# A two-layer decoder trunk in split fp32: seven-product blocks that end with two plain pairs, a gate chain moved into the second block, and another order for the residual adds

## The chip, the cores and the metric

The kernel runs on one core of a Trainium2 chip. The metric is the device time of one execution in microseconds. The profile used here was taken of one execution of the kernel before; times in it are counted from the start of its span. PE is the tensor engine (PEld its weight loads), DVE the vector engine, ACT the scalar engine, POOL GpSimd, SP the engine that issues most of the DMA transfers.

## The reference

The input is 256 tokens of width 2048 in fp32. Layer 0 mixes an mLSTM and a Mamba-2 state-space part behind one combined input projection, layer 1 is attention; each is followed by a SwiGLU of width 5632. Cut to the frame:

```python
for layer in range(DEPTH):
    xn = rms_norm(x, norm_mix[layer])
    if layer % 2 == 0:
        x = x + mixer_mlstm_ssd(xn, *mixer_params[layer])
    else:
        x = x + mixer_moba(xn, *mixer_params[layer])
    x = x + swiglu(rms_norm(x, norm_ffn[layer]), *ffn_params[layer])
return rms_norm(x, final_norm)

def swiglu(x, w_gate, w_up, w_down):
    return (jax.nn.silu(x @ w_gate) * (x @ w_up)) @ w_down
```

In layer 0, `proj = xn @ w_in` holds q, k, v, o of eight mLSTM heads, two gate columns per head, and z, x, B, C and dt of the state-space part. The gates (8 + 8 + 32 columns) go through log-sigmoid, softplus, a running sum and a running maximum before the rest can use them as decays. The two results are joined and go through `w_out`.

## The kernel before

**Blocks.** Every projection is a `block` (L254): 256 tokens against two strips of 512 columns, so four results of 128 tokens x 512 columns in four PSUM banks `F[0..3]` (in the profile `acc_f`). The 2048 rows of a weight matrix are taken in eight pairs of 256 rows (j = 0 to 7). A plan, a string with a letter per pair (`PLAN`, L36), says how a pair is multiplied. Each fp32 factor is split into a high part and a remainder in fp32r, and each product of two such is three matmuls (L262 to L264, `add`).

- P, plain: 4 results x 2 row tiles x 3 = 24 matmuls of 128x512.
- S, seven products (a 2x2 scheme of the Strassen kind): 7 x 3 = 21 matmuls. Three products go straight into `F`, four into extra banks `E` (`acc_e`), which after the last S of the block are folded into four tiles `pre` (L295 on ACT, L296 to L299 on DVE). S needs sums of weights (DVE L244, L246, L247, L249) and sums of activations (`activation_sums`, L210: four small DVE operations on `sf`, then a split on ACT and DVE into `sk`).

**Weights.** `weights` (L226) starts two DMAs of 512 KB per pair from SP, then for every piece a cast on ACT (`wh`, L235) and the remainder on DVE (`wl`, L236). There are 6 buffers each of `raw`, `wh` and `wl`, so the two engines can run ahead of PE only as far as six buffers reach (a P takes two of each, an S four `wh` and four `wl`).

**Sums of activations.** They are made in one of two places: where the activations are turned (`transpose_split`, L187, when pair j is listed in `kt.sums`), or late, when the first S that needs them is reached (`summed`, L178, with an extra add `xg` at L183). In the input `xt0`, in `sx`, `mx` and `o` they are made late; in the inputs of the SwiGLUs (`xt1`, `xt3`), of layer 1 (`xt2`) and in the hidden activations (`ha`, `hb`) where they are turned.

**Order of the work.** Work that belongs to one block and is done during the next is handed to `later` (L142) with a number of pairs to wait; `tick` (L153) runs what is due after every pair, but nothing from the first S of a block to its last (`held`, L139). `need` runs what is still due of a name. A scheduler then orders each engine by the program's order and by the priorities given (`tc.high_priority`: 800 for weights, 1600 for draining banks).

**Blocks in order.** bc0, bc1, xz0 to xz3, qk0 (projection `w_in`), w1.0, w1.1 (`w_out`, state-space half), v0, o0, qk1, v1, o1 (`w_in`), w2.0, w2.1 (`w_out`, mLSTM half), the first SwiGLU (eleven hidden blocks ah0 to ah10, with down blocks ad0, ad4, ad8 of two halves between them), av0, aq0, aq1, av1, aq2, aq3, wo.0, wo.1 (layer 1), and the second SwiGLU (bh0 and so on). These names are the text's; each stands for one call of `block`.

**Around the change.** The gate chain (L432 to L487) stands in line between bc0 and `bc_done(0, FB)` at L562, which drains the banks of bc0 through `scaled` (L537, tile `tok`, on ACT). `project` (L750) adds a `w_out` or `w_o` block to the residual `xin`: `add_all` (L755) adds the four `pre` right after the last S, and the four `F` at the block's end.

Of the kernel before, what the change touches and what calls it, by code (L numbers as in the profile page):

```python
# [60 lines left out]
def hybrid_trunk(ctx: ExitStack, tc: tile.TileContext, a: dict, out: bass.AP):  # L61
# [370 lines left out]
    pg = aux_bank("p_gate")  # L432
    for k in range(KD):
        xh, xl = xt0.parts(k)
        wgh, wgl = wgp[k // 8]
        nc.tensor.matmul(pg[:96, :T], wgh[:, k % 8, :], xh, start=k == 0, stop=False)
        nc.tensor.matmul(pg[:96, :T], wgh[:, k % 8, :], xl, start=False, stop=False)
        nc.tensor.matmul(pg[:96, :T], wgl[:, k % 8, :], xh, start=False, stop=k == KD - 1)
    gate = t2([96, T], "gate")
    nc.vector.tensor_mul(gate, pg[:96, :T], rb0[:96])  # L440
    gv = t2([64, T], "gv")
    nc.vector.tensor_scalar(gv, gate[0:64], gbias[0:64], sgn, op0=OP.add, op1=OP.mult)
    u = t2([8, T], "u")
    nc.vector.tensor_scalar(u, gate[64:72], gbias[64:72], None, op0=OP.add)
    ab = t2([64, T], "ab")
    nc.vector.scalar_tensor_tensor(ab, gv, -1.0, gv, op0=OP.mult, op1=OP.max)
    nc.scalar.activation(ab, ab, AF.Exp, scale=-1.0)
    den = t2([64, T], "den")
    nc.vector.tensor_scalar(den, ab, 2.0, None, op0=OP.add)
    nc.vector.reciprocal(den, den)  # L450
    zz = sk_home([64, 4, T], "zz")
    z, z2, pp, sp = zz[:, 0, :], zz[:, 1, :], zz[:, 2, :], zz[:, 3, :]
    nc.vector.tensor_mul(z, ab, den)
    nc.vector.tensor_mul(z2, z, z)
    nc.vector.tensor_scalar(pp, z2, 1.0 / 17, None, op0=OP.mult)
    for n in (15, 13, 11, 9, 7, 5, 3):
        nc.vector.scalar_tensor_tensor(pp, pp, 1.0 / n, z2, op0=OP.add, op1=OP.mult)
    nc.vector.scalar_tensor_tensor(pp, pp, 1.0, z, op0=OP.add, op1=OP.mult)
    nc.vector.tensor_scalar(gv, gv, 0.0, None, op0=OP.max)
    nc.vector.scalar_tensor_tensor(sp, pp, 2.0, gv, op0=OP.mult, op1=OP.add)  # L460
    ga = t2([64, T], "ga")
    nc.vector.tensor_scalar(ga, sp, lam, None, op0=OP.mult)
    cum = t2([64, T], "cum")
    one_t = t2([64, T], "one_t")
    nc.gpsimd.memset(one_t, 1.0)
    nc.vector.tensor_tensor_scan(cum, one_t, ga, 0.0, op0=OP.mult, op1=OP.add)
    colsrc = t2([P, T], "colsrc")
    nc.gpsimd.memset(colsrc, 0.0)
    nc.vector.tensor_sub(colsrc[0:8], u, cum[0:8])
    cmx = t2([8, T], "cmx")  # L470
    nc.vector.tensor_tensor_scan(cmx, colsrc[0:8], colsrc[0:8], 0.0, op0=OP.max, op1=OP.max)
# [514 lines left out]
```

## Time and profile before

| | us |
|---|---|
| median of 3 runs (2648.64 to 2652.11) | 2651.81 |
| the profiled execution | 2650.01 |
| its span in the trace | 2648.2 |
| PE busy, share of the span | 2572.2, 97% |
| PE weight loads busy | 2106.0, 80% |
| DVE busy | 2284.2, 86% |
| ACT busy | 1528.7, 58% |
| mean DMA rate | 187 GB/s |

A busy PE is not a PE at full pace: matmuls overlap, and at a lower granted clock the same matmul is longer. So the table of busy times says which engines are nearly always occupied, and not how much a stage could give. What a stage could give is read by stretches: the time from the first matmul of a block to that of the next, beside what each engine did in it and the clock that PE was granted. Blocks with the same plan should last the same; where one lasts longer, the timeline of PE shows a start that waited, with the time idle and its releaser in square brackets.

### The profile page before, as it was taken

The page shows a single profiled execution, that of the slowest core. Times are in us where ns is not written, and L with a number is a line of the kernel's source. Part 1 is how long each engine was busy: PE and PEld are TensorE (multiplying, and loading weights), DVE is VectorE, ACT ScalarE, POOL GpSimd, SP SyncE. Part 2 cuts the span into 40 slices and gives each one's busy share as a digit, 9 for nine tenths or more (in the row PEclk, how much of TensorE's full clock was granted, in tenths as well). Part 3 has the DMA queues.
Part 4 walks back from the last instruction along what each step waited for, and adds up shares of the span by engine and source line. Part 5 has one row for each costly group of instructions (what it writes and reads, how often), then busy time and mean ns, then how long its engine had stood idle before and what let it go on. Part 6 is the DMA issues. An engine that isn't in the chain of part 4 may idle for free.

```text
span 2648.2 us, 32709 instructions
## 1 busy us (share of the span) xinstructions
PE 2572.2 (97%) x11630; PEld 2106.0 (80%) x11630; DVE 2284.2 (86%) x3097; ACT 1528.7 (58%) x2052; POOL 59.6 (2%) x97
## 2 busy tenths in 40 slices
...
GB/s 270 138 177 184 184 176 182 183 175 191 179 157 176 192 213 186 202 196 198 190 199 198 187 187 202 146 178 182 140 174 196 196 207 185 207 191 201 198 214 135
DMA packets 254835, 494.51 MB, mean 187 GB/s; under 512 B 16024, under 2 KB 16544, under 8 KB 254672
## 3 DMA queue, kind: packets, MB, share of 16 engines
...
q14 instruction: 72, 0.59, 0.1%
...
## 4 chain that ended last, share of the span: by engine, by line
PE 75%; DVE 11%; issue 8%; DMA 4%; ACT 2%; POOL 1%; ACTq 0%; POOLq 0%; SPq 0%; DVEq 0%
PE acc_f L263 20%; PE acc_f L262 20%; PE acc_f L264 20%; DVE wl L236 5%; PE acc_e L262 4%; PE acc_e L263 4%; PE acc_e L264 4%; ACT wh L235 1%; PE p_tr L192 1%; DMA raw<-in_l_ffn_up 1%; DMA raw<-in_l_ffn_down 1%; DMA raw<-in_l_w_qkv 1%; DVE sums L244 1%; DVE raw L246 1%; DVE sums L247 1%
## 5 line engine op out<-in xcount | busy, mean ns | idle before, releaser
L235 ACT CAST wh<-raw 128x1024 fp32r<-128x1024 f32 (+1 forms) x1049 | 1030.1, 996 | 809.4 <-PE acc_f L264 493.8
L236 DVE TENSOR_TENSOR wl<-raw,wh 128x1024 fp32r<-128x1024 f32 (+1 forms) x1049 | 1197.0, 1151 | 260.2 <-ACT wh L235 252.8
L262 PE MATMUL acc_f<-wh,x 128*128 128x512 f32 x1324 | 520.2, 394 | 9.5 <-DVE xin L757 9.5
L263 PE MATMUL acc_f<-wl,x 128*128 128x512 f32 x1324 | 518.3, 391 | 1.2 <-DVE wl L236 1.2
L264 PE MATMUL acc_f<-wh,x 128*128 128x512 f32 x1324 | 518.5, 392 | 0.0
L262 PEld LDWEIGHTS acc_f<-wh,x 128*128 128x128 f32 x1324 | 249.6, 188 | 61.4 <-issue 6.6
L262 PE MATMUL acc_f<-wh,xa 128*128 128x512 f32 x696 | 278.5, 401 | 15.6 <-ACT tok L537 12.0
L263 PEld LDWEIGHTS acc_f<-wl,x 128*128 128x128 f32 x1324 | 249.7, 189 | 53.9 <-DVE wl L236 3.2
L264 PEld LDWEIGHTS acc_f<-wh,x 128*128 128x128 f32 x1324 | 249.6, 188 | 52.0
L263 PE MATMUL acc_f<-wl,xa 128*128 128x512 f32 x696 | 274.0, 394 | 1.9 <-DVE wl L236 1.9
L264 PE MATMUL acc_f<-wh,xa 128*128 128x512 f32 x696 | 274.4, 394 | 0.0
L236 DVE TENSOR_TENSOR wl<-sums,wh 128x1024 fp32r<-128x1024 f32 x137 | 167.0, 1219 | 9.8 <-ACT wh L235 8.9
L235 ACT CAST wh<-sums 128x1024 fp32r<-128x1024 f32 x137 | 143.7, 1049 | 43.9 <-PE acc_f L264 17.6
L262 PE MATMUL acc_e<-wh,sk 128*128 128x512 f32 x411 | 166.0, 405 | 1.7 <-ACT wh L235 0.8
L262 PEld LDWEIGHTS acc_f<-wh,xa 128*128 128x128 f32 x696 | 131.9, 190 | 43.5 <-ACT tok L537 12.2
L263 PE MATMUL acc_e<-wl,sk 128*128 128x512 f32 x411 | 161.4, 393 | 0.8 <-DVE wl L236 0.8
L264 PE MATMUL acc_e<-wh,sk 128*128 128x512 f32 x411 | 160.2, 392 | 0.0
L263 PEld LDWEIGHTS acc_f<-wl,xa 128*128 128x128 f32 x696 | 131.6, 189 | 28.1 <-DVE wl L236 2.2
L264 PEld LDWEIGHTS acc_f<-wh,xa 128*128 128x128 f32 x696 | 131.5, 189 | 27.2
L244 DVE TENSOR_TENSOR sums<-raw 128x512 f32<-128x512 f32 x137 | 94.0, 686 | 25.9 <-DMA raw<-in_l_w_qkv 6.9
L263 PE MATMUL acc_f<-wl,ha 128*128 128x512 f32 x256 | 100.4, 392 | 3.1 <-DVE wl L236 3.1
L263 PE MATMUL acc_f<-wl,hb 128*128 128x512 f32 x256 | 100.0, 391 | 2.9 <-DVE wl L236 2.9
...
## 6 DMA issues: line engine op xcount, KB each, us to landing
raw<-in_l_w_in SPq DMA_DIRECT2D x192, 512.0 KB, 3.8
...
```

The source lines that it names most:

```text
L192: nc.tensor.transpose(pt[:, i * T + t * P:i * T + (t + 1) * P], src[t][:, i * P:(i + 1) * P], ident)
L235: nc.scalar.copy(h[:, :n, :], of[:, :n, :])
L236: nc.vector.tensor_sub(l[:, :n, :], of[:, :n, :], h[:, :n, :].bitcast(F32))
L244: nc.vector.tensor_sub(sums[:, 0, :], b[:, 1, :], a[:, 1, :])
L246: nc.vector.tensor_sub(b[:, 1, :], b[:, 0, :], b[:, 1, :])
L247: nc.vector.tensor_sub(sums[:, 1, :], b[:, 0, :], sums[:, 0, :])
L262: nc.tensor.matmul(dst, ah, bh, start=start, stop=False)
L263: nc.tensor.matmul(dst, ah, bl, start=False, stop=False)
L264: nc.tensor.matmul(dst, al, bh, start=False, stop=stop)
```

## The change

It has four parts.

1. `PLAN`: in w1.0, w1.1, v0, qk1 and w2.1 the plan PPSPSPSP becomes PSPSPSPP, the plan that the SwiGLU has; in o0, o1, v1, av0 and av1 PPPPSPSP becomes PPPSPSPP; w2.0 goes from three S to two (PPPSPSPP).
2. The gate chain becomes two functions given to `later` with waits of 2 and 6 pairs, so that they run inside bc1; `bc_done(0, FB)` stands before them.
3. `project` has no `add_all`: each `F` is first added to its `pre` (through `gathered`), and `pre` to `xin` after the block at a lower priority.
4. The pairs at which sums of activations are kept and the pools they lie in follow the plans; `x2` keeps three instead of four, and its strips are turned after 1, 2, 1, 2 pairs instead of 1, 3, 1, 3. The three S of v0 and of w1 still make theirs late, as before.

```diff
 PLAN = {
-    "bc": "PPPPPPPP", "xz": "PPPPPPPP", "qk0": "PPPPPPPP", "w1": ("PPSPSPSP", "PPSPSPSP"),
-    "v0": "PPSPSPSP", "o": "PPPPSPSP", "qk1": "PPSPSPSP", "v1": "PPPPSPSP", "w2": ("PPSPSPSP", "PPSPSPSP"),
+    "bc": "PPPPPPPP", "xz": "PPPPPPPP", "qk0": "PPPPPPPP", "w1": ("PSPSPSPP", "PSPSPSPP"),
+    "v0": "PSPSPSPP", "o": "PPPSPSPP", "qk1": "PSPSPSPP", "v1": "PPPSPSPP", "w2": ("PPPSPSPP", "PSPSPSPP"),
     "x": "PSPSPSPP", 4: "PSPSPSPP", 3: "PSPSPP",
-    "av0": "PPPPSPSP", "aq": "PSPSPPPP", "av1": "PPPPSPSP", "wo": ("PPPPPPPP", "PSPSPSPP"),
+    "av0": "PPPSPSPP", "aq": "PSPSPPPP", "av1": "PPPSPSPP", "wo": ("PPPPPPPP", "PSPSPSPP"),
 }
...
+    bc_done(0, FB)
...
-    pg = aux_bank("p_gate")
-    for k in range(KD):
...
+    def gate_chain():
+        pg = aux_bank("p_gate")
+        for k in range(KD):
...
+    later(2, "gates", gate_chain)
+    later(6, "gates", gate_columns)
 
     def decay_rows(first, home):
+        need("gates")
...
-    bc_done(0, FB)
     bc_done(1, bc_block(1))
 
-    sx = KT("sx", KD, s_home, {2: vh_home, 4: vh_home, 6: sk_home})
+    sx = KT("sx", KD, s_home, {1: vh_home, 3: vh_home, 5: sk_home})
...
-            def add_all(what):
-                for i in (0, 2, 1, 3):
-                    nc.vector.tensor_add(dst[i], dst[i], what[i])
-
-            F, _ = block(((w, c0), (w, c0 + STRIP)), kt, row, plans[b], add_all)
-            with tc.high_priority(offset=1600):
-                add_all(F)
+            got = block(((w, c0), (w, c0 + STRIP)), kt, row, plans[b])
+            for t, i, src in gathered(*got):
+                with tc.high_priority(offset=1600 if got[1] is None else 400):
+                    nc.vector.tensor_add(dst[2 * t + i], dst[2 * t + i], src)
...
-    xt2, ss2, finish_ffn0 = next_x("2", G_MIX1, {1: sk_home, 3: sk_home, 4: sk_home, 6: s_home}, (1, 3, 1, 3))
+    xt2, ss2, finish_ffn0 = next_x("2", G_MIX1, {1: sk_home, 3: sk_home, 5: sk_home}, (1, 2, 1, 2))
```

Three places show how the order of instructions moves. The first is ACT from the last pairs of bc0 into bc1; `wh` is a cast of weights, `tok` the drain of bc0's banks, `ab` and `colsrc` are steps of the gate chain, `rb` a row of norms, `cv` a convolution step of the `later` work. Before:

```order
L235 CAST wh<-raw 128x1024 x7
L380 COPY rb_500<-p_rb 128x256
L447 ACTIVATE ab<-ab 64x256
L476 COPY colsrc<-zz 32x256
L475 COPY colsrc<-cum 32x256
L537 ACTIVATE tok<-acc_f,r_489 128x512 x4
L474 ACTIVATE colsrc<-mrow 8x256
L235 CAST wh<-raw 128x1024 x2
```

And after:

```order
L235 CAST wh<-raw 128x1024 x5
L396 ACTIVATE tok<-acc_f,r_489 128x512 x2
L235 CAST wh<-raw 128x1024
L396 ACTIVATE tok<-acc_f,r_489 128x512 x2
L235 CAST wh<-raw 128x1024
L432 COPY rb_500<-p_rb 128x256
L235 CAST wh<-raw 128x1024 x2
L380 ACTIVATE cv<-p_cv,convb,convw 128x256 x2
```

The drain of bc0 no longer stands behind `ab` and `colsrc`; those come later in bc1, one by one between casts of weights.

The second place is DVE at the end of w2.1, the last block before the first SwiGLU; `pre<-pre,acc_e` is the folding of the seven products, `pre<-pre,acc_f` and `xin<-xin,acc_f` read the banks that the next block needs. Before:

```order
L299 TENSOR_TENSOR pre<-pre,acc_e 128x512
L247 TENSOR_TENSOR sums<-raw,sums 128x512
L236 TENSOR_TENSOR wl<-raw,wh 128x1024
L249 TENSOR_TENSOR raw<-raw,sums 128x512
L236 TENSOR_TENSOR wl<-sums,wh 128x1024
L236 TENSOR_TENSOR wl<-raw,wh 128x512
L244 TENSOR_TENSOR sums<-raw 128x512
L757 TENSOR_TENSOR xin_78<-xin_78,pre 128x512
L246 TENSOR_TENSOR raw<-raw 128x512
L757 TENSOR_TENSOR xin_78<-xin_78,acc_f 128x512
```

And after:

```order
L299 TENSOR_TENSOR pre<-pre,acc_e 128x512
L244 TENSOR_TENSOR sums<-raw 128x512
L236 TENSOR_TENSOR wl<-raw,wh 128x1024
L331 TENSOR_TENSOR pre<-pre,acc_f 128x512
L246 TENSOR_TENSOR raw<-raw 128x512
L331 TENSOR_TENSOR pre<-pre,acc_f 128x512
L247 TENSOR_TENSOR sums<-raw,sums 128x512
L331 TENSOR_TENSOR pre<-pre,acc_f 128x512
L236 TENSOR_TENSOR wl<-raw,wh 128x1024
L331 TENSOR_TENSOR pre<-pre,acc_f 128x512
```

Between the last folding and the first read of a bank there stood eight operations, seven of them on weights of S pairs; now there are two, and the adds into `xin` come after all four reads.

The third place is DVE at the start of v0, whose S make their sums of activations late (`xg`, `sf`, `sk`; `xa` is the input turned, `rows` a decay matrix of the mLSTM). Before:

```order
L236 TENSOR_TENSOR wl<-sums,wh 128x1024
L246 TENSOR_TENSOR raw<-raw 128x512
L247 TENSOR_TENSOR sums<-raw,sums 128x512
L236 TENSOR_TENSOR wl<-raw,wh 128x512
L213 TENSOR_TENSOR sf<-xg 128x128
L214 TENSOR_TENSOR sf<-xg 128x128
L215 TENSOR_TENSOR sf<-sf,xg 128x128
L183 TENSOR_TENSOR xg<-xa_261 128x512
```

And after:

```order
L236 TENSOR_TENSOR wl<-sums,wh 128x1024
L246 TENSOR_TENSOR raw<-raw 128x512
L247 TENSOR_TENSOR sums<-raw,sums 128x512
L236 TENSOR_TENSOR wl<-raw,wh 128x512
L765 TENSOR_TENSOR xin_79<-xin_79,pre 128x512
L702 SCALAR_TENSOR_TENSOR rows_4169<-p_s,rows_4169 128x384 x2
L183 TENSOR_TENSOR xg<-xa_115 128x512
L236 TENSOR_TENSOR wl<-raw,wh 128x1024
L213 TENSOR_TENSOR sf<-xg 128x128
```

The first S of v0 now stands one pair earlier, and an add into `xin` and two steps of `rows` stand between its weights and the sums of its activations.

## Rows read from the trace of the kernel before

**Rows 1.** The page: busy time of the engines; the chain of work that ended last, by engine; and the costliest group of instructions, ACT's casts of weights (count, busy time, mean ns of one, idle time before them and what ended most of it).

```profile
PE 2572.2 (97%) x11630; PEld 2106.0 (80%) x11630; DVE 2284.2 (86%) x3097; ACT 1528.7 (58%) x2052; POOL 59.6 (2%) x97
...
PE 75%; DVE 11%; issue 8%; DMA 4%; ACT 2%; POOL 1%; ACTq 0%; POOLq 0%; SPq 0%; DVEq 0%
...
L235 ACT CAST wh<-raw 128x1024 fp32r<-128x1024 f32 (+1 forms) x1049 | 1030.1, 996 | 809.4 <-PE acc_f L264 493.8
```

**Rows 2.** Windows: one stretch per row, its length, then busy time and count of PE, PEld, DVE, ACT and POOL, the granted PE clock (1.00 is full), DMA share and GB/s. These are the stretch of the gate chain, bc1, xz0, and the first five us of bc1.

```profile
58.59:77.05 18.46, 6.48 (x55) 6.24 (x54) 12.66 (x27) 3.28 (x7) 1.14 (x3) 0.77 0.20 59
77.05:128.20 51.15, 51.05 (x226) 41.77 (x227) 32.41 (x48) 27.43 (x38) 4.83 (x7) 0.95 0.58 167
128.20:176.40 48.20, 48.20 (x225) 40.01 (x224) 34.32 (x51) 28.65 (x41) 0.00 (x0) 1.00 0.59 175
77.00:82.00 5.00, 4.85 (x12) 3.46 (x13) 1.72 (x5) 2.15 (x4) 3.87 (x6) 0.50 0.34 73
```

**Rows 3.** Timeline of PE from the last small product of the gate chain into bc1: start, length, what, and in brackets the idle time before it with its releaser.

```profile
64.79 0.28 PE L438 MATMUL p_gate<-xa,wgl 128*96 128x256 f32 x1
77.05 0.80 PE L262 MATMUL acc_f<-wh,xa 128*128 128x512 f32 x1 [11.98 <-ACT tok L537]
77.64 0.63 PE L263 MATMUL acc_f<-wl,xa 128*128 128x512 f32 x1
78.07 0.63 PE L264 MATMUL acc_f<-wh,xa 128*128 128x512 f32 x1
```

**Rows 4.** Timeline of ACT in the same stretch.

```profile
66.89 0.42 ACT L447 ACTIVATE ab<-ab 64x256 f32<-64x256 f32 x1 [6.78 <-DVE ab L446]
74.76 0.40 ACT L476 COPY colsrc<-zz 32x256 f32<-32x256 f32 x1 [7.45 <-DVE zz L460]
...
76.31 2.42 ACT L537 ACTIVATE tok<-acc_f,r 128x512 f32<-128x512 f32 x4
```

**Rows 5.** Windows of single blocks, in this order: ah2 (a SwiGLU block in the steady run), w1.0, w1.1, v0, qk1, w2.0, w2.1, ah0, ad0.1 (a down block), av0, wo.1 and bh0.

```profile
910.46:953.09 42.63, 42.63 (x192) 35.06 (x191) 40.03 (x52) 25.52 (x30) 0.00 (x0) 1.00 0.65 198
389.50:433.63 44.13, 44.07 (x203) 36.23 (x202) 39.25 (x59) 28.35 (x37) 0.00 (x0) 1.00 0.54 173
433.63:478.80 45.17, 42.86 (x184) 34.05 (x183) 39.25 (x49) 23.03 (x27) 1.65 (x4) 1.00 0.65 203
478.80:530.15 51.35, 47.27 (x200) 37.28 (x199) 45.95 (x69) 23.92 (x27) 0.00 (x0) 0.97 0.54 162
577.51:622.92 45.41, 44.24 (x200) 35.54 (x199) 43.06 (x60) 29.88 (x43) 3.13 (x6) 1.00 0.67 206
716.97:769.55 52.58, 47.44 (x201) 36.97 (x199) 48.68 (x74) 29.39 (x39) 0.00 (x0) 0.94 0.49 159
769.55:821.78 52.23, 43.82 (x200) 35.69 (x199) 50.06 (x72) 29.61 (x43) 0.00 (x0) 0.98 0.55 175
821.78:867.78 46.00, 45.99 (x199) 37.51 (x200) 39.71 (x56) 28.98 (x42) 0.70 (x1) 0.95 0.54 165
1038.39:1080.45 42.06, 41.88 (x185) 34.28 (x183) 38.88 (x47) 21.87 (x23) 0.00 (x0) 1.00 0.63 200
1533.62:1578.33 44.71, 44.27 (x204) 36.50 (x203) 40.12 (x66) 28.71 (x44) 1.27 (x1) 1.00 0.54 170
1873.05:1926.55 53.50, 47.56 (x200) 37.53 (x199) 45.73 (x74) 30.45 (x44) 0.00 (x0) 0.94 0.50 157
1926.55:1975.57 49.02, 45.74 (x200) 36.98 (x199) 42.33 (x60) 27.94 (x40) 0.70 (x1) 0.97 0.56 171
```

**Rows 6.** Groups of instructions on DVE, shapes kept apart: line, engine, operation, tiles, count, busy time, mean ns of one, idle time before them and its releasers.

```profile
L236 DVE TENSOR_TENSOR wl<-raw,wh 128x1024 fp32r<-128x1024 f32 x912 | 1103.5, 1221 | 255.6 <-ACT wh L235 248.5 <-DMA raw<-in_l_ffn_down 1.5
L244 DVE TENSOR_TENSOR sums<-raw 128x512 f32<-128x512 f32 x137 | 94.0, 686 | 25.9 <-DMA raw<-in_l_w_qkv 6.9 <-DMA raw<-in_l_ffn_down 4.9 <-DMA raw<-in_l_w_in 4.2
L236 DVE TENSOR_TENSOR wl<-raw,wh 128x512 fp32r<-128x512 f32 x137 | 93.8, 685 | 4.6 <-ACT wh L235 4.3
L133 DVE TENSOR_TENSOR sk<-sf,sk 128x512 fp32r<-128x512 f32 x38 | 26.0, 683 | 0.0
L213 DVE TENSOR_TENSOR sf<-xg 128x128 f32<-128x128 f32 x38 | 10.8, 283 | 0.6 <-ACT xg L201 0.5
```

**Rows 7.** Timeline of PE: two matmuls that follow one another in a block at full clock, then three places at which PE waits (v0, w2.1 to ah0, wo.1).

```profile
1104.04 0.39 PE L262 MATMUL acc_f<-wh,x 128*128 128x512 f32 x1
1104.27 0.39 PE L263 MATMUL acc_f<-wl,x 128*128 128x512 f32 x1
...
504.13 0.50 PE L263 MATMUL acc_f<-wl,xa 128*128 128x512 f32 x1 [1.91 <-DVE wl L236]
...
815.16 0.39 PE L264 MATMUL acc_f<-wh,mx 128*128 128x512 f32 x1
821.78 0.77 PE L262 MATMUL acc_f<-wh,x 128*128 128x512 f32 x1 [6.24 <-DVE xin L757]
...
1889.33 0.47 PE L262 MATMUL acc_e<-wh,o 128*128 128x512 f32 x1 [2.79 <-DVE x L136]
```

**Rows 8.** Timeline of DVE around the start of ah0.

```profile
814.47 0.68 DVE L299 TENSOR_TENSOR pre<-pre,acc_e 128x512 f32<-128x512 f32 x1
815.07 0.69 DVE L247 TENSOR_TENSOR sums<-raw,sums 128x512 f32<-128x512 f32 x1
...
820.96 0.68 DVE L757 TENSOR_TENSOR xin<-xin,acc_f 128x512 f32<-128x512 f32 x1
```

More of the change, by code (lines that the diff above doesn't have):

```diff
@@ L367, in bc_block, with conv_pair @@
         return block(((w_in, C_B + s * STRIP), (w_in, C_C + s * STRIP)), xt0, 0, PLAN["bc"], ready=ready)
+    cb = {}
+    bct = {}
+    def conv_pair(dst, src, ch):
+        pt = aux_bank("p_cv")
+        for i in range(2):
+            for t in range(NT):
+                nc.tensor.transpose(pt[:, i * T + t * P:i * T + (t + 1) * P], src[t][:, i * P:(i + 1) * P], ident)
+        cv = t2([P, 2, T], "cv")
+        for i in range(2):
+            ct = ch + i
+            nc.scalar.activation(cv[:, i, :], pt[:, i * T:(i + 1) * T], AF.Identity, bias=convb[:, ct:ct + 1],
+                                 scale=convw[:, 96 + ct:97 + ct])
+        for i in range(2):
+            ct = ch + i
+            for tap in range(3):
+                sh = 3 - tap
+                nc.vector.scalar_tensor_tensor(cv[:, i, sh:], pt[:, i * T:(i + 1) * T - sh],
+                                               convw[:, 32 * tap + ct:32 * tap + ct + 1], cv[:, i, sh:],
+                                               op0=OP.mult, op1=OP.add)
+        th = t2([P, 2, T], "thc")
+        nc.scalar.activation(th, cv, AF.Tanh)
+        nc.vector.scalar_tensor_tensor(dst, th, 1.0, cv, op0=OP.add, op1=OP.mult)
@@ new lines, in scaled, with bc_done @@
+    def scaled(t, src, r):
+        d = t2([P, STRIP], "tok")
+        with tc.high_priority(offset=1600):
+            nc.scalar.activation(d, src, AF.Copy, scale=r[:, t:t + 1])
+        return d
+    def bc_done(s, got):
+        tok = {}
+        for t, i, src in gathered(*got):
+            tok[i, t] = scaled(t, src, r0_)
+        for i, nm in enumerate("bc"):
+            bct[s, i] = s_home([P, 4, T], f"{nm}T{s}")
+            for j in range(2):
+                later(1 + i, ("bc", s), conv_pair, bct[s, i][:, 2 * j:2 * j + 2, :],
+                      [tok[i, t][:, j * T:(j + 1) * T] for t in range(NT)], 16 + 8 * i + 4 * s + 2 * j)
+        for j in range(2):
+            later(4 + j, "cb", cb_pair, s, j)
@@ L369, in hybrid_trunk, with cb_pair @@
+    def cb_pair(s, j):
+        need(("bc", s))
+        cb[2 * s + j] = s_home([P, 2, W3], "cb")
+        for g in range(2):
+            bT, cT = bct[s, 0][:, 2 * j + g, :], bct[s, 1][:, 2 * j + g, :]
+            pcb = aux_bank("p_cb")
+            nc.tensor.matmul(pcb[:, :T], bT[:, :P], cT, start=True, stop=True)
+            nc.tensor.matmul(pcb[:, T:W3], bT[:, P:], cT[:, P:], start=True, stop=True)
+            nc.scalar.copy(cb[2 * s + j][:, g, :], pcb[:, :W3])
     FB = bc_block(0, input_ready)
@@ L431, in hybrid_trunk @@
         wgp.append((wgh, wgl))
-    pg = aux_bank("p_gate")
-    for k in range(KD):
[L434 to L471, printed above, removed]
@@ L472, in hybrid_trunk @@
-    mrow = t2([8, T], "mrow")
-    nc.vector.tensor_add(mrow, cum[0:8], cmx)
-    nc.scalar.activation(colsrc[96:104], mrow, AF.Exp, scale=-1.0)
-    nc.scalar.copy(colsrc[32:64], cum[32:64])
-    nc.scalar.copy(colsrc[64:96], sp[32:64])
-    nc.vector.tensor_scalar(cum[0:8], cmx, -1.0, None, op0=OP.mult)
-    scr = drp.tile([SH + MH, T], F32, name="scr")
-    nc.gpsimd.dma_start(scr[0:MH], cum[0:8])
-    nc.gpsimd.dma_start(scr[MH:MH + SH], cum[32:64])
-    pc = aux_bank("p_cols")
-    for t in range(NT):
-        nc.tensor.transpose(pc[:, t * P:(t + 1) * P], colsrc[:, t * P:(t + 1) * P], ident)
+    scr = drp.tile([SH + MH, T], F32, name="scr")
@@ L493, in decay_rows, with gate_columns @@
+    def gate_columns():
+        pc = aux_bank("p_cols")
+        for t in range(NT):
+            nc.tensor.transpose(pc[:, t * P:(t + 1) * P], colsrc[:, t * P:(t + 1) * P], ident)
+        nc.vector.tensor_copy(cols, pc[:, :T].rearrange("p (a b) -> p a b", a=NT))
+        nc.vector.tensor_scalar(ncols, cols, -1.0, None, op0=OP.mult)
+    later(2, "gates", gate_chain)
+    later(6, "gates", gate_columns)
     def decay_rows(first, home):
+        need("gates")
         rb = home([P, 2, W3], "rows2")
@@ L534, in scaled @@
-    def scaled(t, src, r):
-        d = t2([P, STRIP], "tok")
-        with tc.high_priority(offset=1600):
-            nc.scalar.activation(d, src, AF.Copy, scale=r[:, t:t + 1])
-        return d
-    def bc_done(s, got):
-        tok = {}
-        for t, i, src in gathered(*got):
-            tok[i, t] = scaled(t, src, r0_)
-        for i, nm in enumerate("bc"):
-            bct[s, i] = s_home([P, 4, T], f"{nm}T{s}")
-            for j in range(2):
-                later(1 + i, ("bc", s), conv_pair, bct[s, i][:, 2 * j:2 * j + 2, :],
-                      [tok[i, t][:, j * T:(j + 1) * T] for t in range(NT)], 16 + 8 * i + 4 * s + 2 * j)
-        for j in range(2):
-            later(4 + j, "cb", cb_pair, s, j)
@@ L552, in cb_pair @@
-    def cb_pair(s, j):
-        need(("bc", s))
-        cb[2 * s + j] = s_home([P, 2, W3], "cb")
-        for g in range(2):
-            bT, cT = bct[s, 0][:, 2 * j + g, :], bct[s, 1][:, 2 * j + g, :]
-            pcb = aux_bank("p_cb")
-            nc.tensor.matmul(pcb[:, :T], bT[:, :P], cT, start=True, stop=True)
-            nc.tensor.matmul(pcb[:, T:W3], bT[:, P:], cT[:, P:], start=True, stop=True)
-            nc.scalar.copy(cb[2 * s + j][:, g, :], pcb[:, :W3])
-    bc_done(0, FB)
     bc_done(1, bc_block(1))
-    sx = KT("sx", KD, s_home, {2: vh_home, 4: vh_home, 6: sk_home})
+    sx = KT("sx", KD, s_home, {1: vh_home, 3: vh_home, 5: sk_home})
```

79 lines of the change are left out of this document (51 added, 28 removed).

## The prediction

> **What bounds the kernel now.** I read the page first: PE is busy 97% of the span, DVE 86%, and the chain that ended last lies on PE for 75%, on DVE for 11% [rows 1]. So PE sets the time nearly everywhere, and DVE sets it in some places. Then the windows block by block. The block to measure others by is ah2: plan PSPSPSPP, 42.63 us, PE busy all of it at clock 1.00, DVE 40.03 busy [rows 5]. At full clock one matmul follows the other by 0.23 us (1104.04 to 1104.27) [rows 7]; the 3 x 21 + 5 x 24 = 183 of a block with three S make 41.6 us, and the rest of ah2 is small products. Blocks of the same work that last longer lose their time to a wait, and the timeline of PE says to which:
>
> - Between bc0 and bc1 PE idles 11.98 us for the drain `tok` [rows 3]. On ACT that drain stands behind two steps of the gate chain, which themselves wait 6.78 and 7.45 us for DVE [rows 4]. The first five us of bc1 then run at clock 0.50 (1.2 GHz instead of 2.4), with matmuls 0.43 apart [rows 2, 3].
> - v0, w2.0 and w2.1 last 51 to 53 us, with DVE busy 46 to 50 of them [rows 5]; PE waits for `wl` there, as at 504.13 [rows 7]. These blocks are at DVE's pace.
> - ah0 begins 6.24 us late: the last matmul of w2.1 started at 815.16, but the bank is free only after DVE's add into `xin` at 820.96 [rows 7, 8].
>
> **The change part by part.** All sums are made against the profiled execution.
>
> *Gate chain.* The stretch from the last bc0 matmul to bc1 is 18.46 us and bc1 itself 51.15 [rows 2], together 69.6. In the new order `tok` stands ahead of the chain, so bc1 starts at once, and its 55 small products (6.48 us of PE [rows 2]) are done inside it. xz0 has the same plan and about as many other small products as bc1 and takes 48.20 at clock 1.00 [rows 2]; 48.20 + 6.48 = 54.7, a gain of 14.9. The chain's DVE work is hidden there: 32.4 + 12.7 = 45.1 us in 54.7 [rows 2]. If the cover fails (chain steps ahead of `wl`, ACT waiting on `ab` ahead of a cast), the waits of 6.78 and 7.45 return once at the worst [rows 4], less what the six weight buffers carry: I bound the gain at 9 to 15.5.
>
> *Plans with two plain pairs at the end.* One S costs DVE four adds of 0.686, three `wl` of 1.22 and a half one of 0.685, 7.1 us; a P costs two `wl`, 2.44 [rows 6]. With PP last, DVE has less to do just when `pre` must be folded and the next block's first weights are due. Where nothing else is late a block should fall to the steady one plus its own small products. By block, each from [rows 5]:
>
> - w1.1, 45.17 of which PE is busy 42.86: ad0.1 has the same matmuls and the new plan, 42.06; -3.1 (bounds -3.5 and 0). w1.0, 44.13, PE busy all of it: 0 (-0.5 and +4: its first S is now a pair earlier).
> - v0, 51.35: it stays at DVE's pace, since three sums of activations are still made late (an `xg` and four `sf`, one `sk`: 0.68 + 4 x 0.28 + 0.68 = 2.5 us each, an add `xg` taken as one of 0.686 [rows 6]). DVE 45.95 plus the 2.6 idle that DVE has in ah2 as well (42.63 - 40.03) make 48.6; I take 49.0, -2.3 (-8 and 0).
> - qk1, 45.41, PE busy 44.24: ah2's 42.63, its eight more small products at 0.9, and a little for late sums; 43.8, -1.6 (-2.1 and +1).
> - w2.0, 52.58: loses one S, 7.1 - 2.4 = 4.7 of its DVE 48.68, for 0.7 of PE (three matmuls). 44.0 + idle of 3.9 as now make 47.9; I take 48.0, -4.6 (-8.5 and 0).
> - w2.1, 52.23 with DVE at 50.06: it now has the sum for pair 1 to make early, beside the turning of the mLSTM's last strips. wo.1 has the very plan and place in layer 1 and takes 53.50, with a wait of 2.79 at the first S [rows 7]. I take 53.0, +0.8 (-9 and +5).
> - o0, o1, v1, av0 and av1 have two S before and after; only their places move. av0 at 44.71 has PE busy 44.27: nothing to gain; 0 together (-1 and +3).
>
> *Residual adds.* Twenty `pre += F` and twenty `xin += pre` take the place of twenty and twenty: 0.68 us each either way [rows 8], so DVE's load is equal. What moves is when a bank is free. Before, eight DVE operations stand between the last folding (814.47) and the first read of a bank (820.96) [rows 8]; now two, and the add into `xin` comes behind. Behind the `pre += F` that waits for PE's last product now stands a `wl` of the next block, which PE reaches later; ah2 has that order and no gap [rows 5]. At ah0 the wait of 6.24 falls to about the one that any block has, but that time counts as the end of w2.1, which I have already priced at DVE's pace; ah0 itself has the slow start (0.77 long instead of 0.39 [rows 7]) off, and the `xin` adds and their transposes later: 47.2 instead of 46.0, +1.2 (-2.5 and +3). bh0, 49.02 at clock 0.97, with DVE busy 42.33: the same order, so 47.2, -1.8 (-5.5 and 0). wo.1 keeps plan and load: 0.
>
> *Counts that change little.* x2 keeps one sum fewer: 2.5 us of DVE, in ad8.1 and av0 where DVE has idle time; 0. No DMA is added, and none is moved past another on SP's queue: the chain's few transfers on POOL only start later, and POOL is busy 2% [rows 1]; their reader is xz1's decay, a block later.
>
> Sum: -14.9 - 3.1 - 2.3 - 1.6 - 4.6 + 0.8 + 1.2 - 1.8 = -26.3. The profiled execution is 2650.0 (span 2648.2 and 1.8 around it), and the median of the runs lies 1.8 above it: 2651.8 - 26.3 = 2625.5; I say 2626.
>
> **The rivals.**
>
> *Only the gate chain gains (2634 to 2642).* In layer 0 DVE's load is almost what it was: of v0, w2.0 and w2.1 only w2.0 loses work. If they run at DVE's pace, order is worth little there. For it: DVE 46 to 50 us of 51 to 53 [rows 5]. Against it: w1.1 and the start of ah0 wait with DVE work that need not stand there. Price: -10 to -18, mean 2638.
>
> *The waits go too (2606 to 2616).* The stalls of v0, w2.0 and w2.1 come from uneven order and not from load, and they fall to about 45 each: -6, -7.5 and -7 instead of -2.3, -4.6 and +0.8, 14.4 more. Against it: a DVE busy 46 to 50 has no room for 45; only w2.0 has its load cut.
>
> *DVE is the bound throughout (2646).* Then the time follows DVE's work. Its counts fall by ten: four of the 0.686 operations, a `wl` of 1.22 and a half one, and some small ones with the sum that x2 drops, about 6.2 us by [rows 6]; the gate chain gives nothing, as its work stays. 2651.8 - 6.2 = 2645.6. Against it: in ah2 PE runs without a gap while DVE has 2.6 us idle, and in bc1 DVE idles 18.7 of 51.15 [rows 2, 5]; DVE's waits ahead of `wl` are 255.6 us, 248.5 of them for ACT's casts [rows 6], and ACT's ahead of those casts 809.4, 493.8 of them for a buffer that PE must free [rows 1]. The Trainium skill (Perfetto Trace Analysis, section Identifying the Most-Contended Engine) tells one to optimize the engine with the highest occupancy first, and to judge the tensor engine by its weight loads and not by its matmul time; by that reading, 80% for PE against 86% for DVE, DVE is the most contended. The trace bears this out in v0, w2.0 and w2.1 alone.
>
> *An early first S that DVE can't serve (slower, 2661).* The plan PSPSPSPP wants the sums of pair 1 some 5.5 us into a block (24 x 0.23), a pair earlier than PPSPSPSP, and in layer 0 they are made late, where DVE also turns strips and scores. wo.1 shows the price, with the same plan: 53.50 against 43.5 (42.63 and its eight more small products, priced at 0.9), 10 lost. The five blocks that get this plan (w1.0, w1.1, v0, qk1, w2.1) would lose 50 in place of the 20.8 that they now lose against 43.5, +29.2, against -20.1 from the gate chain, w2.0, ah0 and bh0: +9. It decides for slower where each of the five loses 6.3 us more than in my sum ((26.3 + 5.3) / 5). Against it: ad0.1 and ah2 run this plan without a loss [rows 5], and the late sums of `xt0` need nothing that is not there.
>
> **How the numbers follow.** My sum 0.52 (2618 to 2634), only the gate 0.19, the waits too 0.13, DVE throughout 0.08, the early S 0.08. Below 2610 lies about a third of the third case and above 2642 the last two, some 0.20 together, so the range is 2610 to 2642. No change means within 0.2%, 5.3 us, which is about what a measurement of this kernel can tell. Above 2646.5 lie about half of the fourth case and all of the fifth, 0.12: 0.07 of it slower than 2657.1, 0.05 between. Faster is 0.88.
>
> **What would show it right or wrong.** In the profile of the changed kernel: the first matmul of bc1 follows bc0's last without a `tok` wait and at clock 1.00, and bc0's end to xz0's start is 54 to 56 us (wrong above 60). w2.0 lasts 47 to 49, v0 48 to 50, w1.1 42 to 43, w2.1 51 to 54. The first matmul of ah0 and of bh0 waits no longer for an add into `xin`. The forecast is wrong if v0 and w2.1 grow with PE waiting for `sk` or `wl` at their first S (the early S), or if w2.0 keeps its 52 (DVE order means nothing), or if `tok` or a cast of bc1 waits behind `ab` or `colsrc` again.

## The result, and the profile after

The changed kernel takes 2627.84 us (median of 4 runs, 2627.04 to 2633.13) against 2651.96 for the kernel before beside it: a ratio of 0.9915, 95% interval 0.9898 to 0.9932. The forecast was 2626 with a range of 2610 to 2642. The profiled execution is 2628.09 us, 21.9 below that of before.

The page of the changed kernel, to set beside [rows 1]:

```profile
PE 2568.4 (98%) x11633; PEld 2103.7 (80%) x11633; DVE 2277.5 (87%) x3087; ACT 1526.4 (58%) x2048; POOL 59.5 (2%) x97
...
PE 78%; DVE 10%; issue 6%; DMA 4%; ACT 1%; POOL 0%; ACTq 0%; SPq 0%; POOLq 0%; DVEq 0%
...
L235 ACT CAST wh<-raw 128x1024 fp32r<-128x1024 f32 (+1 forms) x1048 | 1029.6, 996 | 805.1 <-PE acc_f L264 483.0
```

Work has hardly changed on any engine (DVE 6.7 us less, PE 3.8), yet 21.9 us are gone: they were waits and time at the lower clock. The windows say where. In this order: bc1, xz0, w1.1, v0, qk1, w2.0, w2.1, ah0, bh0, wo.1 and bh8 (the ninth hidden block of the second SwiGLU), columns as in [rows 2] and [rows 5].

```profile
59.34:114.18 54.84, 54.41 (x279) 46.00 (x277) 44.10 (x74) 28.22 (x41) 5.30 (x9) 1.00 0.53 154
114.18:162.36 48.18, 48.18 (x226) 40.01 (x224) 34.31 (x51) 28.64 (x41) 0.80 (x2) 1.00 0.66 200
417.57:459.17 41.60, 41.60 (x185) 34.36 (x184) 37.56 (x46) 22.07 (x23) 1.66 (x4) 1.00 0.67 209
459.17:509.30 50.13, 46.80 (x201) 37.60 (x199) 45.67 (x68) 25.78 (x32) 0.00 (x0) 0.97 0.61 188
556.66:600.17 43.51, 43.51 (x200) 35.80 (x199) 40.54 (x52) 27.60 (x36) 3.12 (x6) 1.00 0.75 234
694.22:739.68 45.46, 44.62 (x203) 36.19 (x202) 41.71 (x62) 25.48 (x33) 0.00 (x0) 1.00 0.54 171
739.68:795.45 55.77, 47.12 (x200) 37.84 (x199) 46.39 (x69) 29.98 (x44) 0.00 (x0) 0.91 0.47 151
795.45:841.32 45.87, 44.45 (x200) 35.35 (x199) 42.27 (x60) 28.49 (x42) 0.70 (x1) 1.00 0.59 184
1902.99:1948.85 45.86, 44.56 (x201) 35.39 (x199) 42.28 (x60) 28.55 (x42) 0.70 (x1) 1.00 0.60 184
1849.36:1902.99 53.63, 47.45 (x201) 37.62 (x199) 45.52 (x74) 30.24 (x44) 0.00 (x0) 0.94 0.51 157
2418.74:2464.99 46.25, 43.79 (x185) 35.37 (x183) 40.02 (x48) 22.86 (x25) 0.00 (x0) 0.96 0.60 182
```

The largest step is at the front. On PE, bc1 now begins right behind the small products that follow bc0, with no bracket and no half clock (compare [rows 3]):

```profile
59.31 0.27 PE L445 MATMUL p_rows<-ident,rows 128*128 128x128 f32 x1
59.34 0.47 PE L262 MATMUL acc_f<-wh,xa 128*128 128x512 f32 x1
```

On ACT three of the four drains are over by then, and the last one runs from 59.07 to 59.76, beside bc1's first matmul and without holding it up. The steps of the gate chain that stood ahead of the drains [rows 4] come 34 us and more after the last of them, and PE has next to no idle time in bc1 (busy 54.41 of 54.84):

```profile
55.05 0.69 ACT L396 ACTIVATE tok<-acc_f,r 128x512 f32<-128x512 f32 x1 [0.32 <-PE acc_f L264]
...
59.07 0.69 ACT L396 ACTIVATE tok<-acc_f,r 128x512 f32<-128x512 f32 x1 [0.51 <-PE acc_f L264]
...
94.06 0.41 ACT L509 ACTIVATE ab<-ab 64x256 f32<-64x256 f32 x1
106.46 0.40 ACT L537 COPY colsrc<-zz 32x256 f32<-32x256 f32 x1
```

At ah0 the wait of 6.24 us [rows 7] is gone too: the last product of w2.1 starts at 795.22 and the first of ah0 at 795.45. Of the blocks with a changed plan w2.1 is the one that grew most, by 3.5 us, and its timeline shows three waits within twelve us. Jobs that turn the strips finished in w2.0 wait for `xin`. The first S, whose `E` bank held a turned strip, waits until DVE has read that bank; and three us on it waits again, for the sum of activations of pair 1, which DVE begins only behind its work on the turned strips:

```profile
753.88 1.09 PE L192 MATMUL p_tr<-ident,xin 128*128 128x128 f32 x8 [1.53 <-DVE xin L765]
761.36 0.77 PE L262 MATMUL acc_e<-wh,mx 128*128 128x512 f32 x1 [6.39 <-DVE x L136]
...
761.93 0.68 DVE L183 TENSOR_TENSOR xg<-mx 128x512 f32<-128x512 f32 x1
...
764.99 0.80 PE L262 MATMUL acc_f<-wh,sk 128*128 128x512 f32 x1 [0.73 <-ACT sk L132]
```

Part of the long wait is ACT's: it makes four squares for the norm, until 756.4, before it reads the first turned strip, and DVE idles 1.79 us for that read.

### The profile page after: what moved, and what is told of

Read it like the earlier page. It is cut to its first block, busy times and chain, and to the rows that moved or that the text cites. A ratio compares the mean times of both kernels' runs of the same rounds, so it can differ in the third digit from the quotient of the medians.

```text
span 2626.3 us, 32711 instructions
## 1 busy us (share of the span) xinstructions
PE 2568.4 (98%) x11633; PEld 2103.7 (80%) x11633; DVE 2277.5 (87%) x3087; ACT 1526.4 (58%) x2048; POOL 59.5 (2%) x97
## 4 chain that ended last, share of the span: by engine, by line
PE 78%; DVE 10%; issue 6%; DMA 4%; ACT 1%; POOL 0%; ACTq 0%; SPq 0%; POOLq 0%; DVEq 0%
PE acc_f L263 21%; PE acc_f L264 21%; PE acc_f L262 20%; DVE wl L236 4%; PE acc_e L262 4%; PE acc_e L264 4%; PE acc_e L263 4%; DMA raw<-in_l_ffn_down 1%; PE p_tr L192 1%; DMA raw<-in_l_ffn_up 1%; DMA raw<-in_l_w_qkv 1%; ACT wh L235 1%; DVE sums L244 1%; DVE xin L817 1%; DVE raw L246 1%
## 5 line engine op out<-in xcount | busy, mean ns | idle before, releaser
L262 PEld LDWEIGHTS acc_f<-wh,x 128*128 128x128 f32 x1324 | 248.4, 188 | 55.8 <-ACT wh L235 3.1
L331 DVE TENSOR_TENSOR pre<-pre,acc_f 128x512 f32<-128x512 f32 x152 | 103.4, 682 | 3.6 <-PE acc_f L264 0.6
```

The source lines that it names most:

```text
L262: nc.tensor.matmul(dst, ah, bh, start=start, stop=False)
L331: nc.vector.tensor_add(pre[i], pre[i], F[i])
```

## The experiments

All are compared with the kernel before on the same chip, in five rounds; differences to the changed kernel are taken between ratios (one interval is about 0.0015 to each side, 4 us, so that a difference of two ratios is known to about 6 us) or between blocks of the profiles, most of which agree to some tenths of a us where nothing is changed. "The changed kernel" is the one of the result.

**The gate chain alone.** The kernel before with part 2 of the change and nothing else:

```diff
+    bc_done(0, FB)
...
+    later(2, "gates", gate_chain)
+    later(6, "gates", gate_columns)
```

> The kernel before with the gate chain moved into bc1 and nothing else changed (plans, adds and sums as before). Theory 1 (PE's waits set the time, and the move takes the 12 us drain wait and the slow clock behind it away): 14 us faster than before, about 2638, xz0 starts at 114 instead of 128, and every later block has its old length. Theory 2 (DVE's work sets the time throughout, the chain's work is only moved): no change, 2652. Theory 3 (the gain is there, but given back in the next blocks, since bc1 now ends with later work): xz0 to qk0 grow by several us and the total gains under 8.

Measured: 2638.66 against 2649.96, ratio 0.9951 (0.9937 to 0.9964), 13.0 us. bc1 of this kernel, and v0:

```profile
59.79:114.63 54.84, 54.42 (x278) 46.01 (x277) 44.11 (x74) 28.23 (x41) 5.31 (x9) 1.00 0.51 155
464.92:516.74 51.82, 48.38 (x201) 38.31 (x200) 45.95 (x69) 24.00 (x27) 0.00 (x0) 0.93 0.52 163
```

xz0 starts at 114.6, 13.6 us earlier. (The two profiles differ by 11.3 at the end: v0, w2.0 and w2.1 are 0.5, 1.4 and 2.2 us longer. Their mean granted clock is lower than before, 0.93, 0.91 and 0.94 against 0.97, 0.94 and 0.98; why is open. So the expectation that every later block keeps its length did not hold there.) The chain's DVE work is all there, so a theory by which time follows DVE's work falls here.

**All but the gate chain.** The changed kernel with the chain in line again, ahead of `bc_done(0, FB)`:

```diff
-    later(2, "gates", gate_chain)
-    later(6, "gates", gate_columns)
+    bc_done(0, FB)
```

> The changed kernel with the gate chain back in line before the drain of bc0 (all else as changed). Theory 1 (gate and the rest add up): 14 us slower than the changed kernel, about 2642, that is 10 us faster than before, and the blocks from w1.0 on as in the changed kernel. If the two parts work only together, it is within 3 us of before or of the changed kernel.

Measured: 2640.72, ratio 0.9966 (0.9952 to 0.9979), 9.0 us faster than before. The wait for `tok` is back (in the list of PE's waits: us in total, times, longest), and w1.1 (41.59) and w2.0 (46.15) are within 0.7 us of the changed kernel:

```profile
PE acc_f L262 <- ACT tok L537: 12.0, 1, 12.0
```

13.0 and 9.0 make 22.0; together they gave 0.85%, 22.5 us. As far as these intervals tell, the two parts add.

**The old order of the residual adds.** The changed kernel with `add_all` in `project`:

```diff
+            def add_all(what):
+                for i in (0, 2, 1, 3):
+                    nc.vector.tensor_add(dst[i], dst[i], what[i])
...
+            F, _ = block(((w, c0), (w, c0 + STRIP)), kt, row, plans[b], add_all)
+            with tc.high_priority(offset=1600):
+                add_all(F)
```

> The changed kernel with the old order of the residual adds (pre into xin after the last S, banks into xin at the end). Theory 1 (the order in which DVE reads the banks counts): the start of bh0 waits for a bank again, bh0 46 to 49 us, and with the ends of w1.1, w2.0, w2.1 and wo.1 the total is 4 to 8 us slower than the changed kernel, 2632 to 2636. Theory 2 (the plans alone did it; with two plain pairs at the end DVE has the time for both orders): within 1.5 us of the changed kernel.

Measured: 2634.46, ratio 0.9944 (0.9932 to 0.9957), 7.7 us slower than the changed kernel by the ratios, 6.4 by the profiles. Its w1.1, w2.1 and bh0:

```profile
417.41:459.01 41.60, 41.60 (x185) 34.37 (x183) 37.59 (x47) 21.89 (x23) 1.66 (x4) 1.00 0.67 209
740.17:798.27 58.10, 48.37 (x200) 38.68 (x199) 47.40 (x70) 29.95 (x44) 0.00 (x0) 0.91 0.44 145
...
1906.71:1955.45 48.74, 45.60 (x200) 36.84 (x199) 42.18 (x60) 27.97 (x40) 0.70 (x1) 0.96 0.53 173
```

bh0 is back at 48.7, with the same DVE work (42.18 against 42.28): its gain of 3.2 us is one of order. PE's matmuls wait again for the adds of `project` into `xin`, 10.3 us in three places; in the changed kernel none of them does. w2.1 is 2.3 us longer and ah0 (47.40) 1.5, and with bh0's 2.9 that is the loss that the profiles show. w1.1 keeps its 41.60: its gain does not need the new order of the adds.

**w2.0 with three S again**, in two ways:

```diff
-"w2": ("PPPSPSPP", "PSPSPSPP")
+"w2": ("PSPSPSPP", "PSPSPSPP")
```

> The changed kernel with three seven-product pairs in w2.0 (PSPSPSPP) instead of two. Theory 1 (w2.0 is at DVE's pace, and an S costs DVE 4.7 us more than a P): w2.0 goes from 45.5 to 49 to 51 us, the total 4 to 5 us slower than the changed kernel. Theory 2 (w2.0 gained by the place of its S and not by the one dropped): w2.0 loses three matmuls, 0.7 us, and stays at 45. Theory 3 (the first S now comes so early that it waits for banks or sums as w2.1's does): over 54 us in w2.0, the total 8 us or more slower.

Measured: 2633.02, ratio 0.9932 (0.9919 to 0.9945), 4.5 us slower than the changed kernel, which the ratios alone do not tell from nothing; the profiles differ by 5.5. w2.0, w2.1 and ah0:

```profile
693.90:751.68 57.78, 50.15 (x201) 37.95 (x199) 50.41 (x76) 28.21 (x37) 0.00 (x0) 0.91 0.47 155
751.68:796.11 44.43, 43.87 (x201) 35.79 (x200) 40.49 (x58) 27.86 (x43) 0.00 (x0) 1.00 0.56 178
796.11:847.02 50.91, 46.51 (x201) 36.67 (x199) 45.05 (x63) 30.43 (x45) 0.70 (x1) 0.97 0.51 165
```

w2.0 grew as theory 3 said (12.3), but the total only as theory 1 said, because w2.1 falls by 11.3 while ah0 grows by 5.0. w2.1 finds its three sums made here, so DVE does 5.9 us less in it, and its first S begins on time. So w2.1's loss in the changed kernel goes where the sum of pair 1 is at hand. But the strips are turned earlier here too, within 7.6 us of the block's start instead of 15.3, so this run alone does not tell the late sum from the bank.

```diff
-"w2": ("PPPSPSPP", "PSPSPSPP")
+"w2": ("PPSPSPSP", "PSPSPSPP")
```

> The changed kernel with w2.0 at the plan it had before (PPSPSPSP, three S, the first at pair 2); w2.1 as changed (PSPSPSPP) has to make its three sums itself. Theory 1 (w2.0 gains by the S that it drops): w2.0 52 to 54 us, as in the kernel before. Theory 2 (by its place and the order of the adds): 48 or less. In the run with three S from pair 1 it took 57.8; so 52 to 54 would put the price of the earlier first S at 4 to 6 us and that of the third S at 7 to 8. w2.1 is 55 to 60 here, and the total 8 to 12 us slower than the changed kernel.

Measured: 2635.32, ratio 0.9942 (0.9929 to 0.9956), 7.2 us slower than the changed kernel. w2.0 and w2.1:

```profile
693.78:743.34 49.56, 46.52 (x200) 36.75 (x199) 45.37 (x71) 26.90 (x35) 0.00 (x0) 0.97 0.46 154
743.34:804.32 60.98, 50.68 (x200) 39.52 (x199) 53.31 (x84) 31.88 (x47) 0.00 (x0) 0.83 0.44 141
```

w2.0 takes 49.6, between the two theories. With the old plan in the new surroundings it is already 3.0 shorter than before (52.58); dropping the third S and starting at pair 3 is worth the other 4.1; and three S from pair 1 on instead of pair 2 cost 8.2. w2.1, at 60.98, is a little above the 55 to 60 that were expected, and the total a little under its 8 to 12.

**w2.1 with two S.** The changed kernel with

```diff
-"w2": ("PPPSPSPP", "PSPSPSPP")
+"w2": ("PPPSPSPP", "PPPSPSPP")
```

> The changed kernel with w2.1 at two seven-product pairs (PPPSPSPP), so that it needs no sum for pair 1 and its first S comes after the strips of w2.0 are turned. Theory 1 (in the changed kernel the first S of w2.1, 12 us late at pair 2, waits for banks that the turned strips hold and for a late sum): w2.1 falls from 55.8 to 45 to 48, the total 7 to 10 us faster than the changed kernel. Theory 2 (w2.1 is at DVE's pace, only load counts): minus 4.7 for the S and 2.5 for the sum, plus 0.7 of PE, at most 6.5 us, and w2.1 stays at 49 or more. Theory 3 (as with the third S of w2.0, the loss only moves on): ah0 grows by 5 us or more and the total gains under 4.

Measured: 2616.68, ratio 0.9872 (0.9852 to 0.9891), 11 us faster than the changed kernel by the ratios, 7.1 by the profiles. w2.1 and ah0:

```profile
740.02:786.88 46.86, 44.86 (x204) 36.22 (x203) 41.98 (x60) 28.07 (x41) 0.00 (x0) 1.00 0.51 169
786.88:832.76 45.88, 44.58 (x201) 35.42 (x200) 42.29 (x60) 28.51 (x42) 0.70 (x1) 1.00 0.58 184
```

8.9 us gone from w2.1, the clock there back at 1.00, and ah0 as it was: the loss did not move on. DVE's work in it fell by only 4.4, and the block lies under the 49 that load alone would have left: about half of the gain is waiting that went, by this reading.

**The strips of w2.0 turned after the last S of w2.1.** Plans, sums and work as in the changed kernel:

```diff
-next_x("1", G_FFN0, {1: vh_home, 3: vh_home, 5: sk_home})
+next_x("1", G_FFN0, {1: vh_home, 3: vh_home, 5: sk_home}, (7, 7, 1, 1))
```

> The changed kernel in which the strips of w2.0 are turned after the last S of w2.1 instead of after its first pair; plans, sums and DVE's work are the same. Theory 1 (the first S of w2.1 waits for banks that the turning holds): w2.1 falls by 6 us or more, and what is turned late costs ah0 or w2.1's end up to 5: the total 2 to 7 us faster than the changed kernel. Theory 2 (DVE's load sets w2.1, order is worth nothing): w2.1 stays within 2 us of 55.8 and the total with it. If the late turning is worse than the wait, ah0 grows by more than w2.1 loses, and the total is slower.

Measured: 2624.83, ratio 0.9906 (0.9889 to 0.9922), not to be told from the changed kernel. w2.1 and ah0:

```profile
740.25:789.84 49.59, 46.90 (x201) 37.41 (x200) 42.31 (x55) 27.35 (x37) 0.00 (x0) 0.93 0.54 171
789.84:842.03 52.19, 47.01 (x201) 36.60 (x199) 47.69 (x75) 31.98 (x50) 0.70 (x1) 0.97 0.49 161
```

w2.1 loses 6.2 us and the wait of 6.39 for the bank is not in the trace any more; ah0 grows by 6.3, with 5.4 us more DVE work. In w2.1 DVE has 4.1 us less to do (42.31 against 46.39), and the sum of pair 1 is made with no turning ahead of it. So the run shows that the loss goes when the turning does, and that moving the turning only moves the work to the next tight place; it does not tell apart the bank, the late sum and the load.

**The gains of the final norm in other buffers.** bh8 is 4.1 us longer in the changed kernel than in the one before, though nothing in its code changed. DVE waits there for weights:

```profile
2419.49 0.69 DVE L244 TENSOR_TENSOR sums<-raw 128x512 f32<-128x512 f32 x1 [2.70 <-DMA raw<-in_l_ffn_up]
```

and the four loads of the final norm's gains on ACT's queue (L944, 256 KB each), which in the kernel before started at 2545.5 to 2552.9 (late in the second SwiGLU), stand just ahead of it, with a longer time to landing:

```profile
L944 ACTq DMA_DIRECT2D gf<-in_final_norm x4: 334/390/456, 2397.9 to 2408.4; - x4
...
DMA to landing us min/median/max: 5.5/6.8/8.1
```

Part 4 of the change moved other tiles between the pools, and a buffer of `sk` came free earlier. The experiment takes the gains' buffers from the pool `vh`, which is free only late:

```diff
-            gain["pair"] = sk_home([P, 2, STRIP], "gf")
+            gain["pair"] = vh_home([P, 2, STRIP], "gf")
```

> The changed kernel in which the gains of the final norm lie in the pool of vh tiles instead of sk, so that their four loads start at 2520 to 2540 us, as in the kernel before, and not at 2398 to 2408, where the weights of bh8 are loading. Theory 1 (bh8's 4 us over its like are the loads' doing): bh8 falls from 46.2 to 42.2 to 42.8, nothing else changes, the total 3 to 4 us faster than the changed kernel. Theory 2 (bh8's extra is chance or something else): within 1 us of the changed kernel, and bh8 stays at 46.

Measured: 2620.15, ratio 0.9886 (0.9871 to 0.9901). The loads start at 2515.5 and land after 4.4 us, and bh8 is

```profile
2415.03:2457.11 42.08, 41.89 (x185) 34.30 (x184) 38.15 (x46) 22.98 (x25) 0.00 (x0) 1.00 0.63 200
```

4.2 us shorter. The profiles differ by 8.1 in all, about twice what was expected; the rest is small steps in a dozen blocks that the edit does not touch (ad8.1 1.6, av0 and bh0 about 1 each), and the ratios do not tell 4 from 8.

**v0 and qk1 with two S.** The changed kernel with

```diff
-"v0": "PSPSPSPP"
+"v0": "PPPSPSPP"
...
-"qk1": "PSPSPSPP"
+"qk1": "PPPSPSPP"
```

> The changed kernel with v0 and qk1 at two seven-product pairs (PPPSPSPP), so that the sum of pair 1 of the input is made nowhere after w1. Theory 1 (v0 is at DVE's pace: its load falls by 4.7 for the S and 2.5 for the sum): v0 falls from 50.1 to 44 to 46; qk1, which waits for nothing now, gains nothing and loses the three matmuls (0.7): the total 3 to 5 us faster than the changed kernel. Theory 2 (v0's loss is one of order): v0 keeps 48 or more and the total is within 2 us.

Measured: 2619.91, ratio 0.9884 (0.987 to 0.9899), 8 us faster by the ratios. v0 and qk1:

```profile
460.00:504.88 44.88, 44.88 (x203) 37.33 (x202) 40.50 (x57) 22.90 (x26) 0.00 (x0) 1.00 0.60 188
552.24:596.24 44.00, 44.00 (x204) 36.47 (x202) 39.11 (x53) 28.43 (x42) 3.12 (x6) 1.00 0.68 210
```

v0 loses 5.2 us of time for 5.2 of DVE work, and qk1 grows by half a us, about the matmuls it now has more: qk1 waited for nothing. In v0 what went were waits for weights (3.3 us) and 3.4 us at half the granted clock behind them. That fits DVE's pace; but the S given up is also the early one, so the run takes load and order away together. The two blocks make 4.8 of the 8; bh8 (44.2), ah0 and bh0 are 2.0, 0.9 and 0.9 shorter as well, which the edit does not explain.

**All of it.** w2.1, v0, qk1 and also wo.1 at PPPSPSPP, and the gains in `vh`:

> The changed kernel with what the last runs point to, together: w2.1, v0 and qk1 at two seven-product pairs (PPPSPSPP), wo.1 too, and the gains of the final norm in the pool of vh tiles. Theory 1 (the losses are separate places, each a wait at an early first S or a load in the wrong place, and they add): w2.1 -9, v0 -5, bh8 -4, and wo.1, which has the plan and the wait of w2.1, from 53.6 to 46 or 47, -7: 25 us faster than the changed kernel, about 2603, 1.8% faster than before. Theory 2 (DVE's load is what is saved: four S dropped at 4.7 and four late sums at 2.5, less 0.7 of PE each): also about -25 where the block is at DVE's pace, but wo.1 stays at 48 or more, as 45.7 of DVE less 7.2 and 7.8 of idle make 46 only if the wait goes as well. Theory 3 (they share one reserve of DVE and don't add): 10 to 15 us faster than the changed kernel, with bh0 or ah0 longer.

Measured: 2599.61 us, ratio 0.981 (0.9797 to 0.9824): 1.9% faster than the kernel before and 1.05% faster than the changed one, 28 us. v0, w2.1, wo.1 and bh8:

```profile
459.70:504.58 44.88, 44.88 (x204) 37.32 (x202) 40.39 (x57) 23.01 (x26) 0.00 (x0) 1.00 0.60 189
735.90:781.68 45.78, 44.68 (x203) 36.28 (x202) 40.94 (x59) 28.09 (x41) 0.00 (x0) 1.00 0.52 169
1835.16:1881.26 46.10, 44.57 (x203) 36.46 (x202) 41.51 (x66) 27.36 (x40) 0.00 (x0) 1.00 0.52 171
2395.52:2437.62 42.10, 41.91 (x184) 34.28 (x183) 38.16 (x46) 22.97 (x25) 0.00 (x0) 1.00 0.63 200
```

v0 -5.3, w2.1 -10.0, wo.1 -7.5 and bh8 -4.2 make 27.0 of the 27.8 between the two spans: the places are separate and add. wo.1 falls below the 48 of theory 2, by more than its DVE work does (45.52 to 41.51), so its wait went as well. The four S given up cost PE twelve matmuls, 2.8 us at 0.23 each. This is the fastest version of the study.

## Why the prediction was right, point by point

The sum was -26.3 on the profiled execution, and -21.9 came (-22.5 by the ratio). The mechanism was right for the larger part, the gate chain; that the total lies so near is partly luck, as the misses go both ways: w2.0, ah0 and bh0 gained 5.2 more than forecast, and w2.1, v0 and the blocks priced at nothing lost 9.5. By its terms, each the difference of two windows (forecast, then measured):

| term | forecast | measured |
|---|---|---|
| gate chain and bc1, by the start of xz0 | -14.9 | -14.0 |
| w1.1 | -3.1 | -3.6 |
| v0 | -2.3 | -1.2 |
| qk1 | -1.6 | -1.9 |
| w2.0 | -4.6 | -7.1 |
| w2.1 | +0.8 | +3.5 |
| ah0 | +1.2 | -0.1 |
| bh0 | -1.8 | -3.2 |
| all these | -26.3 | -27.6 |
| blocks priced at nothing | 0 | +5.7 |

- *Gate chain.* Right in mechanism and size: bc1 is 54.84 where xz0 plus its small products made 54.7. The cover held (DVE busy 44.10 of it). The run with the chain alone shows it by itself.
- *w1.1 and qk1.* Right: both now have PE busy all of their time, as ah2 has. The run with the old adds shows that w1.1 does not owe it to them.
- *v0.* The working came out near; DVE's idle time is 4.5 where I took ah2's 2.6. The run with two S fits DVE's pace with 5.2 us of time for 5.2 of work, but it drops the early first S too, so order is not excluded.
- *w2.0.* Mis-sized: I took the dropped S off DVE (4.7) and not the late sum that goes with it, which I had priced at 2.5 in the term of v0. 48.68 - 7.2 is 41.5, and DVE is busy 41.71. That this fits so well is partly chance: in the run with the old plan in w2.0 the block has the same three S as before and DVE is busy 45.37, 3.3 less, as fourteen whole remainders `wl<-raw` fall into its stretch instead of seventeen. The plans of the blocks around it shift work across its edges.
- *w2.1.* I priced the late sum by DVE's load and wo.1's whole time. The load fell (50.06 to 46.39) and the block still grew: its first S needs a bank in which a strip is being turned, 6.39 us, then the late sum of pair 1, which came at 764.99, and the clock was at half from 758.5 to 768.8. Had the bank been free at once, the sum would still have been missing; no run parts the two. This is the rival of the early first S, in the place where it said DVE turns strips, and right in one block of the five that it named: in w1.0 (43.93 of 43.93), w1.1 and qk1 PE is busy all of the time, and in v0 it waits for weights (1.1 us at the longest), not for a bank.
- *ah0 and bh0.* The reads of the banks came before the adds into `xin`, as read from the order; I allowed too much for the later adds. The run with the old adds gives bh0's part back.
- *Priced at nothing.* bh8 +4.1 (the gains' loads), av0 +1.6 and aq2 +2.4 against av1 -2.3 (small products that had run in av1 now run in aq2), ad8.1 +2.5, ah1 +0.8, ad4.1 -3.3 and qk0 -1.8. Of these bh8's cause is shown. ad4.1 and ad8.1 move by 2 to 3 us between runs that don't touch them, and the clock moves with them (ad4.1 0.96 before and 1.00 after, ad8.1 1.00 and 0.95); what starts it isn't settled; nor was it tried what of av0's is x2's changed waits. Nearly 2 us more are 0.13 in each of some fifteen SwiGLU blocks in their steady run (ah2 42.63 before, 42.77 after), in every run with the new plans and not in the one with the gate chain alone; which part does it is open.

Of the signs that the prediction named, the gate chain's all came (bc0's end to xz0's start is 55 us), and neither ah0 nor bh0 waits for an add into `xin`. The lengths all missed their narrow ranges: w2.0 at 45.5 (47 to 49), v0 at 50.1 (48 to 50), w1.1 at 41.6 (42 to 43) and w2.1 at 55.8 (51 to 54).

Of the rivals, "only the gate chain" falls with the run without it (9.0 us are left), and "DVE is the bound throughout" with the chain alone (13 us for no DVE work saved). "The waits go too" put v0, w2.0 and w2.1 at about 45 each, and only w2.0 came there; in the best version all three lie between 44.9 and 45.9. The Trainium skill's reading of the rival of DVE (Perfetto Trace Analysis, section Identifying the Most-Contended Engine) is borne out by this trace at most within v0 and w2.0 (7.1 us of time for 7.0 of DVE's); between the changed kernel and the best one DVE's busy time falls by 22.5 us (2277.5 to 2255.0) for 27.8 us of span, between before and the changed kernel by 6.7 for 21.9.
